# A hybrid pooling and short-convolution block on one core: the order of the branch units, a product by way of DRAM, and two Strassen steps more

## The chip, the cores and the metric

The kernel runs on one core of one Trainium2 chip. The metric is the device time of one execution in microseconds (us); lower is better. The engines are named as in the profile: PE (TensorE, matrix products), DVE (VectorE), ACT (ScalarE), POOL (GpSimd) and SP (SyncE); the last two issue transfers here, and POOL does little else.

## The reference

256 tokens, a model width of 4096, all in float32. The weights are read once and dominate the data (about 470 MB for the input, branch and output products).

```
h    = rmsnorm(x, norm_w)
proj = h @ w_in                      # 4096 -> 20480, split into u_p, z_p, u_c, b_c, c_c, z_c, g_logit
y_pool = causal_multiscale_pool(u_p) * silu(z_p)     # 2048 channels
y_conv = causal_gated_shortconv(u_c, b_c, c_c) * silu(z_c)   # 2048 channels
br     = [y_pool @ w_branch[0], y_conv @ w_branch[1]]        # each 2048 -> 4096
gates  = sigmoid(g_logit + gate_b)                   # two gates of 4096
merged = gates[0] * br[0] + gates[1] * br[1]
out    = rmsnorm(x + merged @ w_out, final_norm_w)
```

## The kernel before

**Units and steps.** Every large product is cut into units of 1024 output columns. A unit goes through its input channels in steps of 256 channels: 16 steps for the input and the output products, 8 steps for a branch product. A step loads 1 MB of weights into one of three `raw` buffers (SP issues the load), splits them into a high and a low part in the `ring` (ACT rounds the high part, DVE subtracts to get the low part), and multiplies by the standing operand, which lies in the `arena` in the same two parts. A product of two numbers is three matmuls: high by high, high by low, low by high.

**Two kinds of step.** A `P` step is the plain 2 by 2 block product: 8 block products, 24 matmuls of 128x512. An `S` step is one level of a Strassen scheme: 7 block products, 21 matmuls. It needs four sums of weight blocks as well (`parts`, made on DVE and split like the weights), and its products go to four more PSUM banks (`shared`, beside `sums`). When the unit ends, ACT copies those four into the tile `J` and DVE makes corner sums of them (`corner_sums`: three instructions), and the sums are added into the unit's result, `E` or `Y` (`combine`). A string of `P` and `S` sets the kinds and their order in each unit: `TEN`, for example, has ten `S`.

**How the corners are added.** Where `u.late` is set, POOL adds `J` to the result by two accumulating transfers (`gather`); otherwise DVE adds them, `E<-E,J` for a branch unit.

**The ring.** It has 15 cells of 512 columns. A `P` step takes 4 cells, an `S` step 3 and then 4 more for the sums. A cell comes free when PE has done its last matmul with it. So DVE and ACT work about two steps ahead of PE.

**What sets the order.** All engines run their instructions in the order in which the program is written (`pin` keeps it). After each group of matmuls, `pump` writes the preparation of later steps, and every 6 matmuls is a tick: one item is taken from a `queue`, which holds the epilogue of the unit before (`epi`, with `None` for an empty tick), and fills of standing operands may move on (`pop_fill`: POOL fetches a piece into `sa`, `sb` or `sc`, DVE and ACT make the operand of it).

**Branch units.** `b0_c` is gate column block c of branch zero, `b1_c` of branch one, c from 0 to 3. The order is b0_0, b1_0, b0_1, b1_1, b0_2, b1_2, b0_3, b1_3. `b0_c` ends with `Y = E * Y`, where Y held gate zero. `b1_c` ends with `E = E * gate one` (line 722; gate one lies in the tile `last_pair`, which the program calls `spare()`), `E = E + Y`, eight transposes of E on PE in each of two ticks, and a store of the turned result to `m_d[c]`, which the output units read. The gates of c = 0 stay in SBUF, the others are fetched from `gates_d`. The unit after b1_c thus carries its epilogue: in its first PE steps stand the transposes, which wait for the DVE instruction `E<-E,Y`.

**What the change touches.** The unit g1_0 (the last of the input product, text `SEVEN3`), `branch_unit` and the loop that makes the branch units.

Of the kernel before, what the change touches and what calls it, by code (L numbers as in the profile page):

```python
# [9 lines left out]
F32 = mybir.dt.float32  # L10
# [5 lines left out]
P = 128  # L16
# [3 lines left out]
NU = 1024  # L20
NH = 512
# [12 lines left out]
SIX5 = "PPPPPSPSPSPSPSPS"  # L34
FIRST = (0, 1, 8, 2, 9, 3, 10, 11, 4, 12, 13, 5, 14, 6, 15, 7)
OPENED = 12
SEVEN3 = "PPPSPSPSPSPSPSPS"
NINE = "PSPSPSPSSPSPSSPS"
NINE_A = "PSPSSPSPSSPSPSPS"
NINE_P = "PSPSSPSPSSPSSPSP"  # L40
HOST = "PPBPPMMPSSPSSPSSPSS"
TEN = "PSPSSPSSPSSPSSPS"
OUT3 = "PSPSPSPSPSPSSPPP"
B0 = "PPPPSPSP"
B1 = "PSPSPSPP"
B1_FIRST = "PPSPSPSP"
B0_MORE = "PPPPSSPS"


@with_exitstack  # L50
def hybrid_block(ctx: ExitStack, tc: tile.TileContext, x, xc, prm, rows_in, w_in, pool_w, w_branch, w_out, out):
# [5 lines left out]
    def act(dst, src, func=AF.Copy, **kw):  # L57
        return pin(nc.scalar.activation(dst, src, func, **kw))  # L58

    def tt(dst, a, b, op):  # L60
        return pin(nc.vector.tensor_tensor(out=dst, in0=a, in1=b, op=op))  # L61

    def mul(dst, a, b):
        return tt(dst, a, b, ALU.mult)

    def add(dst, a, b):
        return tt(dst, a, b, ALU.add)
# [13 lines left out]
    def move(dst, src):  # L81
        return pin(nc.gpsimd.dma_start(dst, src))

    def gather(dst, src):
        return pin(nc.gpsimd.dma_start(dst, src, accum_op=ALU.add))  # L85
# [5 lines left out]
    dram = ctx.enter_context(tc.tile_pool(name="dram", bufs=1, space=bass.MemoryType.DRAM))  # L91

    def sb(name, shape, dt=F32):
        return upper.tile(shape, dt, name=name)

    def blocks(name, shape, dt=F32):
        return const.tile(shape, dt, name=name)
# [4 lines left out]
    E = blocks("E", [P, 2, NU])  # L102
    sa = blocks("sa", [P, 8, P])
    J = blocks("J", [P, 4, NH])
    ident = blocks("ident", [P, P])
    raw = sb("raw", [P, NRAW, 2 * NU])
    Y = sb("Y", [P, 2, NU])
# [10 lines left out]
    gates_d = dram.tile([2, 4, P, 2, NU], F32, name="gates_d")  # L118
    g_d = dram.tile([2, P, 2, NU], F32, name="g_d")
    side_d = dram.tile([2, P, 2, 4, P], F32R, name="side_d")  # L120
    y_d = dram.tile([2, 2, P, 4, 2, T], F32, name="y_d")
    m_d = dram.tile([4, P, 4, 2, T], F32, name="m_d")
    o_d = dram.tile([3, P, 2, NU], F32, name="o_d")

# [28 lines left out]
    def open_last(dt):  # L153
        stack = ExitStack()
        ctx.enter_context(stack)
        pool = stack.enter_context(tc.tile_pool(name="last", bufs=1, side="right"))
        last_pair.update(stack=stack, tile=pool.tile([P, 8 * KB], dt, name="last_pair"))
# [87 lines left out]
    def quarters(tile_):  # L245
        return tile_.rearrange("p a (b c) -> p (a b) c", c=NH)
# [154 lines left out]
    def shared(i):  # L401
        return PF[i]
# [52 lines left out]
    def transposes(src, done):  # L455
        items = []
        for j in range(4):
            def f(j=j):
                for i in range(2):
                    for t in range(2):  # L460
                        c = (2 * j + i) * P
                        pin(nc.tensor.transpose(shared(j)[:, i * T + t * P:i * T + (t + 1) * P],  # L462
                                                src[:, t, c:c + P], ident))
                done(j)
            items.append(f)
        return items

    def pairs(items):
        return [lambda a=a, b=b: (a(), b()) for a, b in zip(items[::2], items[1::2])]

    def put(dst, src):
        for k in range(2):
            move(dst[:, :, 1 - k], src.rearrange("p (q k) t -> p q k t", k=2)[:, :, k])

    def chan(tile_):
        return tile_.rearrange("p a n -> p (a n)").rearrange("p (b t) -> p b t", t=T)

    def bankview(j):
        return shared(j).rearrange("p (b t) -> p b t", t=T)

    def gap(n):
        return [None] * n
# [36 lines left out]
    def seq_y(text):  # L519
        return sequence(text, 8 - text.count("S"), 8, 0)  # L520

    def in_unit(name, col, epi, text, **kw):
        units.append(Unit(name, lambda i: w_in[col // NU, i], seq_x(text), x_ops, epi, scaled=True, **kw))
        units[-1].text = text
        return units[-1]
# [20 lines left out]
    def rescale(d):  # L546
        return gap(18) + [lambda: act(d[:, 0], d[:, 0], scale=rin[:, 0:1]), None,
                          lambda: act(d[:, 1], d[:, 1], scale=rin[:, 1:2])]
# [142 lines left out]
    def gate_unit(n, c):  # L691
        first, final = (n, c) == (0, 0), (n, c) == (1, 0)

        def epi(u):
            d = u.dst

            def bias(t):
                gather(d[:, t], gate_b[n, None, c * NU:(c + 1) * NU].to_broadcast([P, NU]))

            def gate(t):  # L700
                act((spare() if final else d)[:, t], d[:, t], AF.Sigmoid)

            items = (rescale(d) if u.late else gap(1)) + [lambda: bias(0), lambda: bias(1)] + gap(12) + [
                lambda: gate(0), None, lambda: gate(1)]
            return items if first or final else items + [lambda: move(gates_d[n, c], E)]
        text = HOST if first else SEVEN3 if final else TEN
        u = in_unit(f"g{n}_{c}", 6 * HALF + n * D + c * NU, epi, text, dst=Y if first else E)
        u.late = not final

    def spare():  # L710
        return last_pair["tile"].rearrange("p (a n) -> p a n", a=2)

    def branch_unit(n, c):
        def epi(u):
            if n == 0:
                if c:
                    return gap(10) + [lambda: move(spare(), gates_d[1, c])] + gap(8) + [lambda: mul(Y, E, Y)]
                return gap(8) + [lambda: mul(Y, E, Y)]
            turned = spare() if c < 3 else Y

            def gated():
                mul(E, E, spare())
                if c == 3:
                    last_pair["stack"].close()
                    open_last(F32R)
                    last_pair["again"] = True

            def copy(j):
                act(chan(turned)[:, 2 * j:2 * j + 2], bankview(j))

            def stored():
                put(m_d[c], chan(turned))
                merged[c] = now[0] + STORED
            return gap(2) + [gated, None, lambda: add(E, E, Y), None,
                lambda: c < 3 and move(Y, gates_d[0, c + 1])] + gap(4) + pairs(transposes(E, copy)) + [stored]

        text = (B1 if c else B1_FIRST) if n else B0_MORE if c else B0
        u = Unit(f"b{n}_{c}", lambda i: w_branch[n, c, i], seq_y(text), y_ops[n], epi)
        u.late = n == 0 and c > 0
        if not u.late:  # L740
            u.urgent, u.lead = (lambda: None), 3
        units.append(u)
# [86 lines left out]
    for c in range(2):  # L829
        pool_units(c)  # L830
    gate_unit(0, 0)
    for c in range(1, 4):
        for n in range(2):
            gate_unit(n, c)
    gate_unit(1, 0)
    last_x = units[-1]
    for c in range(4):
        branch_unit(0, c)
        branch_unit(1, c)
    for c in range(4):  # L840
        out_unit(c)

# [126 lines left out]
    def done(i):  # L969
        steps[i].prepared = True  # L970
# [184 lines left out]
    for st in lead:  # L1155
# [7 lines left out]
        if not combined and last.closed(FB):  # L1163
            combined = True
            flush()
            rest = sums.rearrange("p (t a) n -> p t (a n)", t=2)
# [80 lines left out]
```

## Time and profile before

| what | value |
|---|---|
| median of 3 runs | 2356.45 us (2356.26 to 2356.69) |
| the profiled execution | 2356.82 us, of which the span of the instructions is 2354.7 us |
| PE busy | 2340.7 us (99%), 10,424 matmuls |
| DVE busy | 2217.8 us (94%) |
| ACT busy | 1542.9 us (66%) |
| POOL busy | 139.0 us (6%) |
| DMA | 569.44 MB, mean 242 GB/s |

In the rows of the profile, L61 is every DVE tensor-by-tensor operation, L58 every ACT operation, L82 and L85 the plain and the accumulating transfers of POOL, L1026 the matmuls of the steps and L462 the transposes. A row of the timeline gives the start, the time, the engine, the line and `out<-in`; in square brackets stand the idle time before it and what ended it. Two DVE rows that follow each other overlap by about 0.08 us in the records, so a piece's cost is taken from start to start.

### The profile page before, as it was taken

What the parts mean: (1) busy time and instruction counts of PE and PEld (TensorE: products, weight loads), DVE (VectorE), ACT (ScalarE), POOL (GpSimd) and SP (SyncE); (2) the same over time, 40 slices, a digit from 0 to 9 for tenths busy, and PEclk for the clock granted to TensorE, in tenths of its full rate; (3) what the DMA queues carried; (4) which work ended last, traced back from release to release, by engine and by line L of the source; (5) the groups of instructions that cost most, each with busy time, mean ns of one, the idle gap of its engine ahead of it and who ended that gap; (6) DMA issues with size and microseconds to landing.
All of it is one profiled execution on the core that took longest, in us unless ns stands there. A gap on an engine that the chain in (4) does not pass through costs nothing.

```text
span 2354.7 us, 28337 instructions
## 1 busy us (share of the span) xinstructions
PE 2340.7 (99%) x10424; PEld 1938.7 (82%) x10424; DVE 2217.8 (94%) x2454; ACT 1542.9 (66%) x1841; POOL 139.0 (6%) x195
## 2 busy tenths in 40 slices
PE   9999999999999999999999999999999999999998
PEld 7888888888888888888888888888888888888886
DVE  8899989999979979979999999998999899999998
ACT  6666756766656666666677767677666566566664
POOL 0000000000001000100000000001101001000000
PEclk9999999999999999999999999999999999999999
DMA  9667655776656656656787787778767678767877
GB/s 351 231 234 248 217 201 215 251 232 233 222 207 216 219 196 213 220 198 222 242 258 254 256 265 246 250 267 283 258 225 247 254 247 282 250 206 263 260 255 279
DMA packets 95387, 569.44 MB, mean 242 GB/s; under 512 B 10320, under 2 KB 10576, under 8 KB 34832
## 3 DMA queue, kind: packets, MB, share of 16 engines
q1 hardware_dynamic: 69824, 485.39, 56.7%
q0 software_dynamic: 24848, 81.01, 13.7%
q8 instruction: 81, 1.33, 0.2%
q10 hardware_dynamic: 576, 1.24, 0.1%
q14 instruction: 58, 0.48, 0.1%
HBM read 521.46 MB, written 25.17 MB: 232 GB/s over the span
## 4 chain that ended last, share of the span: by engine, by line
PE 97%; DVE 1%; DMA 0%; ACT 0%; issue 0%; DVEq 0%; SPq 0%; ACTq 0%
PE sums L1026 70%; PE shared L1026 25%; PE shared L676 1%; PE shared L462 1%; DVE ring L61 1%; DMA raw<-in_w_branch_dram 0%; DVE parts L61 0%; DMA raw<-in_w_in_dram 0%; ACT ring L58 0%; DVE arena L61 0%; PE shared L652 0%; DVE J L61 0%; ACT E L58 0%; PE shared L653 0%; PE shared L655 0%
## 5 line engine op out<-in xcount | busy, mean ns | idle before, releaser
L1026 PE MATMUL sums<-ring,arena 128*128 128x512 f32 x7011 | 1640.7, 390 | 1.9 <-ACT E L58 1.1
L1026 PEld LDWEIGHTS sums<-ring,arena 128*128 128x128 f32 x7011 | 1315.3, 188 | 275.5 <-ACT E L58 1.5
L61 DVE TENSOR_TENSOR ring<-raw,ring 128x1024 fp32r<-128x1024 f32 (+2 forms) x887 | 962.2, 1104 | 70.4 <-ACT ring L58 69.5
L58 ACT ACTIVATE ring<-raw 128x1024 fp32r<-128x1024 f32 (+3 forms) x682 | 785.5, 1192 | 210.2 <-PE sums L1026 98.5
L58 ACT ACTIVATE ring<-parts 128x512 fp32r<-128x512 f32 (+1 forms) x683 | 510.4, 761 | 510.2 <-DVE parts L61 438.3
L1026 PE MATMUL shared<-ring,arena 128*128 128x512 f32 x2241 | 541.1, 389 | 0.0
L61 DVE TENSOR_TENSOR ring<-parts,ring 128x1024 fp32r<-128x1024 f32 (+1 forms) x475 | 524.5, 1146 | 8.7 <-ACT ring L58 8.7
L1026 PEld LDWEIGHTS shared<-ring,arena 128*128 128x128 f32 x2241 | 420.6, 188 | 87.3
L61 DVE TENSOR_TENSOR parts<-parts,raw 128x512 f32<-128x512 f32 x444 | 303.3, 683 | 0.0
L61 DVE TENSOR_TENSOR parts<-raw 128x1024 f32<-128x1024 f32 x222 | 270.2, 1217 | 10.9 <-DMA raw<-in_w_in_dram 6.0
L61 DVE TENSOR_TENSOR J<-J 128x512 f32<-128x512 f32 (+1 forms) x90 | 78.1, 868 | 6.0 <-ACT J L58 2.8
L1026 PE MATMUL sums<-ring,last_pair 128*128 128x512 f32 x306 | 76.2, 389 | 0.0
L58 ACT ACTIVATE J<-shared 128x512 f32<-128x512 f32 x128 | 69.5, 601 | 1.6
L1026 PEld LDWEIGHTS sums<-ring,last_pair 128*128 128x128 f32 x306 | 57.4, 188 | 11.9
L85 POOL DMA_DIRECT2D E<-J x28 | 34.2, 1463 | 479.5 <-ACT ring L58 300.1
L1026 PE MATMUL shared<-ring,last_pair 128*128 128x512 f32 x216 | 51.9, 389 | 0.0
L1026 PE MATMUL shared<-ring,side 128*128 128x512 f32 x207 | 50.7, 389 | 0.0
L1026 PEld LDWEIGHTS shared<-ring,last_pair 128*128 128x128 f32 x216 | 40.5, 188 | 8.4
L1026 PEld LDWEIGHTS shared<-ring,side 128*128 128x128 f32 x207 | 38.9, 188 | 8.1
L58 ACT ACTIVATE E<-sums 128x512 f32<-128x512 f32 x76 | 41.8, 592 | 4.5 <-PE sums L1026 2.7
L85 POOL DMA_DIRECT2D Y<-J x12 | 14.7, 1458 | 265.1 <-ACT ring L58 138.5
L58 ACT ACTIVATE E<-sums,rin 128x512 f32<-128x512 f32 x20 | 13.0, 689 | 13.9 <-PE sums L1026 13.9
(140 smaller groups left out, 645.6 us busy)
## 6 DMA issues: line engine op xcount, KB each, us to landing
raw<-in_w_in_dram SPq DMA_DIRECT2D x318, 1024.0 KB, 4.9
raw<-in_w_branch_dram SPq DMA_DIRECT2D x64, 1024.0 KB, 5.4
raw<-in_w_out_dram SPq DMA_DIRECT2D x64, 1024.0 KB, 4.8
E<-J POOLq DMA_DIRECT2D x28, 512.0 KB, 8.6
E<-in_rows_dram POOLq DMA_DIRECT2D x14, 512.0 KB, 9.8
Y<-J POOLq DMA_DIRECT2D x12, 512.0 KB, 9.3
gates_d<-E POOLq DMA_DIRECT2D x6, 1024.0 KB, 6.1
y_d<-E POOLq DMA_DIRECT2D x8, 512.0 KB, 5.2
```

The costliest lines, as they stand in the source:

```text
L58: return pin(nc.scalar.activation(dst, src, func, **kw))
L61: return pin(nc.vector.tensor_tensor(out=dst, in0=a, in1=b, op=op))
L85: return pin(nc.gpsimd.dma_start(dst, src, accum_op=ALU.add))
L462: pin(nc.tensor.transpose(shared(j)[:, i * T + t * P:i * T + (t + 1) * P], src[:, t, c:c + P], ident))
L676: pin(nc.tensor.matmul(o, a, b, start=(k, i) == (0, 0), stop=(k, i) == (3, 2)))
L1026: pin(nc.tensor.matmul(ps, lhs, rhs, start=n == 0, stop=n == u.total[b] - 1))
```

## The change

The unit g1_0 gets eight `S` steps in place of seven. The branch units run in the order b0_0, b0_1, b1_0, b1_1, b0_2, b1_2, b0_3, b1_3. All units of branch zero, b0_0 now among them, take the text PPPPSSPS and have their corners added by transfers; b0_0 had PPPPSPSP, so it has three `S` in place of two. b1_0 changes from PPSPSPSP to PSPSPSPP, and b1_1 from PSPSPSPP to PPPPSSPS, each with three `S` as before. The first product of branch zero is stored to a new DRAM tile `p_d` while b0_1 runs, and Y takes gate zero of c = 1 after it. b1_0's epilogue loads `p_d` into J and adds J where it added Y. Gate one of c = 1 is fetched at the end of that epilogue, and no longer during b0_1.

```diff
-SEVEN3 = "PPPSPSPSPSPSPSPS"
+EIGHT3 = "PPPSPSPSSPSPSSPS"
...
-B0 = "PPPPSPSP"
 B1 = "PSPSPSPP"
-B1_FIRST = "PPSPSPSP"
-B0_MORE = "PPPPSSPS"
+B_LATE = "PPPPSSPS"
...
+    p_d = dram.tile([P, 2, NU], F32, name="p_d")
...
-        text = HOST if first else SEVEN3 if final else TEN
+        text = HOST if first else EIGHT3 if final else TEN
...
     def branch_unit(n, c):
         def epi(u):
             if n == 0:
-                if c:
-                    return gap(10) + [lambda: move(spare(), gates_d[1, c])] + gap(8) + [lambda: mul(Y, E, Y)]
-                return gap(8) + [lambda: mul(Y, E, Y)]
+                product = gap(18) + [lambda: mul(Y, E, Y)]
+                if c == 0:
+                    return product + [None, lambda: move(p_d, Y), lambda: move(Y, gates_d[0, 1])]
+                if c > 1:
+                    product[10] = lambda: move(spare(), gates_d[1, c])
+                return product
...
-            return gap(2) + [gated, None, lambda: add(E, E, Y), None,
-                lambda: c < 3 and move(Y, gates_d[0, c + 1])] + gap(4) + pairs(transposes(E, copy)) + [stored]
-
-        text = (B1 if c else B1_FIRST) if n else B0_MORE if c else B0
+            head = gap(2) + [gated, None, lambda: add(E, E, Y), None,
+                             lambda: c < 3 and move(Y, gates_d[0, c + 1])] + gap(4)
+            rest = []
+            if c == 0:
+                head = [lambda: move(J, p_d.rearrange("p a (b n) -> p (a b) n", n=NH)), None, gated] + gap(4) + [
+                    lambda: add(quarters(E), quarters(E), J)] + gap(3)
+                rest = gap(7) + [lambda: move(spare(), gates_d[1, 1])]
+            return head + pairs(transposes(E, copy)) + [stored] + rest
+
+        text = B1 if n and c != 1 else B_LATE
         u = Unit(f"b{n}_{c}", lambda i: w_branch[n, c, i], seq_y(text), y_ops[n], epi)
-        u.late = n == 0 and c > 0
+        u.late = n == 0
...
-    for c in range(4):
-        branch_unit(0, c)
-        branch_unit(1, c)
+    for n, c in ((0, 0), (0, 1), (1, 0), (1, 1), (0, 2), (1, 2), (0, 3), (1, 3)):
+        branch_unit(n, c)
```

The rows below are the program's order as it is built, without times; `x2` is the same row twice. First VectorE where the unit after b1_1, which is b0_2 in both kernels, begins. `J<-J` are b1_1's corner sums, `E<-E,J` adds them, `E<-E,last_pair` is the product with gate one, `parts` and the rows between belong to b0_2's first `S` step, and `E<-E,Y` is what the transposes wait for. Before:

```order
L61 TENSOR_TENSOR J<-J 128x512 x2
L61 TENSOR_TENSOR J<-J 128x1024
L61 TENSOR_TENSOR ring<-raw,ring 128x4x512 x2
L61 TENSOR_TENSOR E<-E,J 128x2048
L61 TENSOR_TENSOR ring<-raw,ring 128x4x512
L61 TENSOR_TENSOR E<-E,last_pair 128x2048
L61 TENSOR_TENSOR parts<-raw 128x1024
L61 TENSOR_TENSOR ring<-raw,ring 128x512
L61 TENSOR_TENSOR parts<-parts,raw 128x512
L61 TENSOR_TENSOR ring<-raw,ring 128x2x512
L61 TENSOR_TENSOR parts<-parts,raw 128x512
L61 TENSOR_TENSOR E<-E,Y 128x2048
```

The same place on VectorE now:

```order
L59 TENSOR_TENSOR ring<-raw,ring 128x4x512 x2
L59 TENSOR_TENSOR J<-J 128x512 x2
L59 TENSOR_TENSOR J<-J 128x1024
L59 TENSOR_TENSOR E<-E,J 128x2048
L59 TENSOR_TENSOR ring<-raw,ring 128x4x512
L59 TENSOR_TENSOR E<-E,last_pair 128x2048
L59 TENSOR_TENSOR parts<-raw 128x1024
L59 TENSOR_TENSOR ring<-raw,ring 128x512
L59 TENSOR_TENSOR parts<-parts,raw 128x512
L59 TENSOR_TENSOR ring<-raw,ring 128x2x512
L59 TENSOR_TENSOR parts<-parts,raw 128x512
L59 TENSOR_TENSOR E<-E,Y 128x2048
```

b1_1 ended in two `P` steps and ends in an `S` step now: its corner sums moved behind the preparation of two of b0_2's `P` steps, and from `E<-E,J` on the rows are the same. The place of the transposes on PE is the same too, 69 matmuls into b0_2.

Then POOL's queue from b0_0's end to b1_1's, before:

```order
L82 DMA Y<-gates_d 128x2048
L82 DMA m_d<-last_pair 512x1x256 x2
L82 DMA sa<-m_d 128x512
L82 DMA sb<-m_d 128x512
L82 DMA sc<-m_d 128x512
L85 DMA E<-J 128x2x512 x2
L82 DMA last_pair<-gates_d 128x2048
L82 DMA Y<-gates_d 128x2048
```

The same stretch of POOL's queue now:

```order
L83 DMA E<-J 128x2x512 x2
L80 DMA p_d<-Y 128x2048
L80 DMA Y<-gates_d 128x2048
L83 DMA E<-J 128x2x512 x2
L80 DMA J<-p_d 128x2048
L80 DMA m_d<-last_pair 512x1x256 x2
L80 DMA sa<-m_d 128x512
L80 DMA sb<-m_d 128x512
L80 DMA last_pair<-gates_d 128x2048
L80 DMA sc<-m_d 128x512
L80 DMA Y<-gates_d 128x2048
```

New are b0_0's two accumulating transfers, the store of the product and the load of it into J; the fetch of gate one moved behind the store of `m_d[0]`.

## The prediction

> **What bounds the kernel now.** I read the page first: engine shares, then the chain that ended last.
>
> ```profile
> PE 2340.7 (99%) x10424; PEld 1938.7 (82%) x10424; DVE 2217.8 (94%) x2454; ACT 1542.9 (66%) x1841; POOL 139.0 (6%) x195
> PE 97%; DVE 1%; DMA 0%; ACT 0%; issue 0%; DVEq 0%; SPq 0%; ACTq 0%
> ```
>
> PE is on the path nearly everywhere. A busy PE need not be at its pace, so I took that from the busy times by stretch, one stretch per unit from its first matmul to the next unit's: g1_1, g1_0, b0_0, b1_0, b0_2.
>
> ```profile
> core 0: us, PE busy (x) PEld busy (x) DVE busy (x) ACT busy (x) POOL busy (x), PEclk, DMA share, GB/s
> 1191.43:1271.67 80.24, 80.24 (x356) 66.44 (x354) 80.17 (x90) 56.51 (x69) 5.29 (x6) 1.00 0.80 258
> 1592.63:1674.91 82.28, 82.28 (x365) 68.13 (x363) 74.89 (x87) 55.69 (x66) 10.28 (x15) 1.00 0.84 275
> 1674.91:1718.30 43.39, 42.32 (x188) 34.72 (x186) 41.66 (x51) 31.20 (x39) 5.06 (x8) 1.00 0.80 263
> 1718.30:1759.95 41.65, 41.65 (x183) 34.47 (x184) 40.69 (x44) 27.27 (x34) 0.00 (x0) 1.00 0.55 202
> 1844.73:1888.03 43.30, 43.30 (x200) 36.01 (x199) 37.79 (x37) 25.85 (x33) 2.06 (x3) 1.00 0.67 242
> ```
>
> g1_1 has 10 S and 6 P, 10 x 21 + 6 x 24 = 354 matmuls in 80.24 us: 226.7 ns each. g1_0's 363 take 82.28 us, the same pace, without a gap. b0_0's 186 would take 42.16 us and take 43.39, b1_0's 183 would take 41.48 and take 41.65. So the branch part loses 1.23 + 0.17 = 1.40 us at one place, which PE's waits name (in us, times, longest), the only one of them behind the program's first 6 us:
>
> ```profile
> PE sums L1026 <- ACT E L58: 1.1, 1, 1.1
> ```
>
> It is the start of b1_0; the timeline of ACT and PE there:
>
> ```profile
> 1715.76 1.49 ACT L58 ACTIVATE ring<-raw 128x1536 fp32r<-128x1536 f32 x1 [1.29 <-DMA raw<-in_w_branch_dram]
> 1717.15 0.61 ACT L58 ACTIVATE arena<-sb 128x512 fp32r<-128x512 f32 x1
> 1717.67 2.04 ACT L58 ACTIVATE E<-sums 128x512 f32<-128x512 f32 x4
> 1718.30 1.45 PE L1026 MATMUL sums<-ring,arena 128*128 128x512 f32 x5 [1.07 <-ACT E L58]
> ```
>
> b0_0 ends in a P step, which closes its four `sums` banks together; their copies stood on ACT behind a piece that had waited for a load.
>
> So a reduction of work elsewhere than on PE is worth nothing. The change can gain only its matmuls and this wait, and lose whatever wait it makes.
>
> **The matmuls.** Two units trade a P for an S: 2 x (24 - 21) = 6 matmuls x 226.7 ns = -1.36 us.
>
> **The old wait.** b0_0 now ends in an S, in which the `sums` banks close up to a whole step before the end, and b0_1 follows. Taken as gone: -1.40 us; nothing saved if it comes back.
>
> **What the trades cost DVE.** The timeline of DVE at the start of b0_2, after b1_1, which has all pieces:
>
> ```profile
> 1845.56 2.29 DVE L61 TENSOR_TENSOR E<-E,J 128x2048 f32<-128x2048 f32 x1 [0.46 <-ACT E L58]
> 1848.24 2.29 DVE L61 TENSOR_TENSOR ring<-raw,ring 128x2048 fp32r<-128x2048 f32 x1 [0.39 <-ACT ring L58]
> 1850.45 2.29 DVE L61 TENSOR_TENSOR E<-E,last_pair 128x2048 f32<-128x2048 f32 x1
> 1852.65 1.22 DVE L61 TENSOR_TENSOR parts<-raw 128x1024 f32<-128x1024 f32 x1
> ...
> 1856.73 2.28 DVE L61 TENSOR_TENSOR E<-E,Y 128x2048 f32<-128x2048 f32 x1
> 1858.93 2.35 DVE L61 TENSOR_TENSOR ring<-parts,ring 128x1024 fp32r<-128x1024 f32 x2
> 1861.20 1.21 DVE L61 TENSOR_TENSOR parts<-raw 128x1024 f32<-128x1024 f32 x1
> ```
>
> From start to start, a P's preparation is 2.2 us, and an S's 1856.73 - 1852.65 = 4.1 for the sums and 1861.20 - 1858.93 = 2.3 for their split, 6.4 together: +4.2 us of DVE per trade. In g1_0 DVE is busy 74.9 of 82.3 us, so 7.4 us of idle time take it; g1_1 keeps PE's pace with ten S and DVE at 80.17 of 80.24. Cost in g1_0: 0.
>
> In b0_0 it is closer. g1_0's own epilogue and six fills fall there; DVE's timeline at its start:
>
> ```profile
> 1677.90 2.29 DVE L61 TENSOR_TENSOR ring<-raw,ring 128x2048 fp32r<-128x2048 f32 x1 [1.20 <-ACT ring L58]
> 1680.11 2.67 DVE L61 TENSOR_TENSOR J<-J 128x512 f32<-128x512 f32 x3
> 1682.81 2.48 DVE L73 SCALAR_TENSOR_TENSOR E<-J,rin,E 128x1024 f32<-128x1024 f32 x2
> 1685.21 1.22 DVE L61 TENSOR_TENSOR ring<-raw,ring 128x1024 fp32r<-128x1024 f32 x1
> ```
>
> And the groups of the fills' pieces (count, busy time, mean ns):
>
> ```profile
> L61 DVE TENSOR_TENSOR sa<-sa 128x128 f32<-128x128 f32 x68 | 16.6, 286 | 0.8 <-ACT sa L58 0.2
> L61 DVE TENSOR_TENSOR arena<-sa,arena 128x896 fp32r<-128x896 f32 x11 | 12.0, 1089 | 0.2
> L61 DVE TENSOR_TENSOR arena<-sa,arena 128x512 fp32r<-128x512 f32 x7 | 4.8, 682 | 0.0
> ```
>
> DVE is done with the third P's piece 5.2 us after b0_0's first matmul (1674.91). The 1.2 us of idle time before it, ended by ACT, show that DVE was not late, so the extra S of g1_0 doesn't move it. From there, in the new order up to the sums of the last S: corners and their addition 5.1 (1680.11 to 1685.21), two P 4.4, three S 19.1, and fills: twelve small sums at 16.6 / 68 = 0.24, two pieces of 0.6, one of 1.0 and one of 1.1 (a `parts` row above): 6.2. Together 5.2 + 34.8 = 40.0 us. PE needs the last of these sums in the third product of that step: 4 x 24 + 2 x 21 + 24 + 7 = 169 matmuls, 38.3 us. A wait of 1.7; 0.7 if ACT, which has one fill piece less to do ahead of that P than in the trace, lets DVE start 1 us sooner. Bounds 0 and 2.0; I take +0.8, near the sooner start, whose cause stands in the built order.
>
> **The new wait: b0_2's transposes.** In the rows above, b1_1's corner sums were over before b0_2 began (they are not in the list), `E<-E,J` ended at 1847.85, 3.1 us after b0_2's first matmul at 1844.73, and `E<-E,Y` at 1859.01, 14.3 us after it. The transposes follow:
>
> ```profile
> 1842.69 17.85 PE L1026 MATMUL sums<-ring,arena 128*128 128x512 f32 x78
> 1860.38 1.03 PE L462 MATMUL shared<-ident,E 128*128 128x128 f32 x8
> ```
>
> They start 15.65 us after it (69 matmuls), 1.4 us after DVE was done. b1_1 now ends in an S, whose `shared` banks close last: its corner sums come after two P pieces of b0_2, as g1_0's stand behind those of b0_0 in the trace. There the corners are over 1682.81 - 1674.91 = 7.9 us into the unit, since the second P's rounding on ACT stands between the copies of `J`:
>
> ```profile
> 1674.44 0.65 ACT L58 ACTIVATE arena<-sb 128x512 fp32r<-128x512 f32 x1
> 1674.96 1.10 ACT L58 ACTIVATE J<-shared 128x512 f32<-128x512 f32 x2
> 1675.92 1.95 ACT L58 ACTIVATE ring<-raw 128x2048 fp32r<-128x2048 f32 x1
> 1677.72 1.11 ACT L58 ACTIVATE J<-shared 128x512 f32<-128x512 f32 x2
> ```
>
> Without that fill (0.5) and with slightly shorter copies of `E` I take 7.1. Then `E<-E,J` 2.2, a P 2.2, gate one 2.2, the sums of the S 4.1, `E<-E,Y` 2.3: 20.1. PE waits 20.1 - 15.65 = 4.4 us. Bounds: 3.2, if the corners begin as soon as ACT's last copy is done (3.2, and 2.7 for them, so 5.9), and 5.2 with g1_0's 7.9. Nothing hides it: PE has no idle time to give back.
>
> **The transfers.** The issues (count, KB each, median us from issue to landing):
>
> ```profile
> gates_d<-E POOLq DMA_DIRECT2D x6, 1024.0 KB, 6.1
> Y<-gates_d POOLq DMA_DIRECT2D x3, 1024.0 KB, 5.6
> last_pair<-gates_d POOLq DMA_DIRECT2D x3, 1024.0 KB, 17.6
> ```
>
> The product of b0_0 comes 18 ticks (24.5 us) into b0_1 at the earliest, say at 30. Store 6.1 and load of Y 5.6 on POOL: 42. Behind them in the queue stand b0_1's own `E<-J`, which have no corners before 46, and Y is read 24 us into b1_0: 0, with 20 us of cover. `J<-p_d` can start when `E<-E,J` is done, 3.1 us into b1_1 (P ends b1_0, as it ended b1_1 above), and lands near 9; DVE comes to its `E<-E,J` at 12, and the transposes at 72 matmuls, 16.3, leave 2.0 more. Cost 0 as long as the load takes under 10.5 us. The fills of y for b1_0 have a unit more. The addition in b1_0's epilogue replaces another; b0_0's corners leave DVE (2.2 us) for transfers that end long before tick 18.
>
> **Sum.** -1.36 - 1.40 + 0.8 + 4.4 = +2.4 us. The profiled execution took 2356.82 us around its span of 2354.7, 0.37 over the median of 2356.45, to which I apply the sum: 2358.9 us, +0.10%. A measurement of this kernel tells about 0.2% from no change, 4.7 us: 2351.7 to 2361.2. Faster than that is not in PE's reach, as only 2.8 us can be gained.
>
> **Rivals.** *No new wait.* If b1_1's corners are done as early as after a P, the 1.4 us of slack stay: 2356.45 - 2.76 = 2353.7. Against it: the S closes those banks last, and g1_0 shows 7.9 us. 8%.
>
> *The stall stops the clock.* The busy times at the program's end (the granted clock is the third number from the right):
>
> ```profile
> 2335.00:2344.00 9.00, 8.72 (x39) 6.89 (x37) 7.24 (x16) 3.54 (x8) 0.00 (x0) 1.00 0.32 130
> 2344.00:2349.00 5.00, 0.00 (x0) 0.00 (x0) 4.17 (x11) 2.08 (x4) 0.00 (x0) 0.94 0.67 270
> 2349.00:2354.00 5.00, 0.00 (x0) 0.00 (x0) 0.00 (x0) 0.00 (x0) 0.00 (x0) 0.50 0.87 356
> ```
>
> And PE's timeline at its start:
>
> ```profile
> 5.98 6.35 PE L1026 MATMUL sums<-ring,arena 128*128 128x512 f32 x18 [0.83 <-DVE ring L774]
> ```
>
> PE ends at 2343.7; a mean of 0.94 over 5 us is 0.6 us at half clock, so it fell at 2348.4, 4.7 us after the last matmul. And 18 matmuls at the start took 6.35 us where they take 4.2 at pace: 2.1 us lost. If the stall at the transposes reaches 4.7 us (its upper bound is 5.2), the clock falls and PE restarts slowly: 2356.45 - 2.76 + 0.8 + 5.2 + 2.1 = 2361.8, slower. Against it: my 4.4 is below, and the wait of 1.07 us at 1718 left the clock at 1.00. 13%. [...]
>
> *J comes late.* At 17.6 us, as `last_pair<-gates_d`, it lands 21.1 into b1_1, DVE's addition ends at 23.4 and PE waits 7.1 more: 2366. Against it: those loads stood behind two accumulating transfers, and this one has none ahead. 4%.
>
> *DVE falls behind by more in g1_0 or b0_0.* For it: in b0_0 the running sum has no idle time left, so any delay there is PE's. Against it: g1_1 holds the pace with ten S. 3 us over my sum would be 2361.9. 5%.
>
> **Chances and range.** The forecast has 70%; its own range is 2356.45 - 2.76 + 3.2 = 2356.9 to 2356.45 - 2.76 + 2.0 + 5.2 = 2360.9. The range 2355.5 to 2361.9 leaves out the case without a wait, the late J and the upper halves of the clock and DVE cases. Faster 1%; within 0.2% the forecast and the first rival, 78%; slower 21%.
>
> **What would show it.** Right: the unit g1_0 at 360 x 226.7 ns = 81.6 us; no wait for `E<-sums` copies at the unit after b0_0; PE waiting for DVE's `E` 3 to 5 us ahead of the transposes in b0_2, with `E<-E,Y` ending near 20 us into it; under 2 us of waiting for DVE's `ring` at b0_0's last S; J landing 9 us into b1_1. Wrong: transposes in b0_2 that wait for nothing, a wait in b1_1, or a granted clock under 1.00 after the stall.

## The result, and the profile after

| | before | after |
|---|---|---|
| median, same chip | 2356.82 us (2356.09 to 2357.91, 10 runs) | 2362.82 us (2362.36 to 2365.21, 10 runs) |
| ratio to before | | 1.0026, 95% interval 1.0018 to 1.0034 |
| profiled execution, span | 2356.82, 2354.7 us | 2362.69, 2361.0 us |

The change makes the kernel 6.0 us slower; +2.4 was forecast. (Two single executions in the experiments, one of e12 with 3972.29 us and one of the kernel before beside it with 4827.55 us, are left out of all numbers.) In the kernel after, the step matmuls stand at L1033, the transposes at L461, DVE's operations at L59 and ACT's at L56. PE's waits (us in total, times, longest) first; the row of `ring` at L59 also holds a wait in the first 20 us:

```profile
PE shared L461 <- DVE E L59: 4.3, 1, 4.3
PE sums L1033 <- DVE ring L59: 2.8, 2, 1.8
PE sums L1033 <- ACT E L56: 1.0, 1, 1.0
```

The busy times by stretch, one stretch per unit: g1_0, b0_0, b0_1, b1_0, b0_2 (columns as in the prediction):

```profile
1593.13:1674.73 81.60, 81.60 (x361) 67.57 (x360) 78.45 (x92) 57.77 (x68) 10.29 (x15) 1.00 0.84 266
1674.73:1718.64 43.91, 41.95 (x185) 34.08 (x183) 41.99 (x53) 29.41 (x35) 4.34 (x7) 1.00 0.73 241
1718.64:1760.56 41.92, 41.90 (x184) 34.38 (x185) 40.93 (x44) 28.63 (x36) 4.30 (x6) 1.00 0.89 287
1760.56:1802.04 41.48, 41.48 (x185) 34.35 (x184) 39.04 (x37) 27.34 (x32) 2.44 (x2) 1.00 0.81 267
1845.34:1894.70 49.36, 45.11 (x200) 37.24 (x199) 42.37 (x42) 28.16 (x35) 2.02 (x3) 0.97 0.62 216
```

g1_0 is 0.68 us shorter, as 3 matmuls of 226.7 ns should make it. A branch unit of three `S` that waits for nothing takes 41.48 (b1_0); the transposes bring it to 43.30. So b0_0 loses 2.43 us, b0_1 0.44 and b0_2 6.06. That b0_2's granted clock is 0.97, not 1.00, is the second thing to see.

DVE at the start of b0_2, then PE there:

```profile
1849.65 2.67 DVE L59 TENSOR_TENSOR J<-J 128x512 f32<-128x512 f32 x3
1852.36 2.29 DVE L59 TENSOR_TENSOR E<-E,J 128x2048 f32<-128x2048 f32 x1
...
1856.77 2.28 DVE L59 TENSOR_TENSOR E<-E,last_pair 128x2048 f32<-128x2048 f32 x1
1858.97 1.21 DVE L59 TENSOR_TENSOR parts<-raw 128x1024 f32<-128x1024 f32 x1
...
1863.06 2.28 DVE L59 TENSOR_TENSOR E<-E,Y 128x2048 f32<-128x2048 f32 x1
```

```profile
1845.34 15.80 PE L1033 MATMUL sums<-ring,arena 128*128 128x512 f32 x69
1865.39 1.66 PE L461 MATMUL shared<-ident,E 128*128 128x128 f32 x8 [4.25 <-DVE E L59]
```

The corners end 7.0 us into the unit (7.1 forecast), `E<-E,Y` 20.0 (20.1), and the transposes start 4.4 us later than 69 matmuls would let them. The rest of the 6.06, 1.66 us, is the clock. The busy times in three stretches of 3.41 us that begin within the stall (the granted clock is the third number from the right):

```profile
1862.35:1865.76 3.41, 0.37 (x3) 0.37 (x4) 3.41 (x4) 2.00 (x2) 0.12 (x1) 1.00 0.42 120
1865.76:1869.17 3.41, 3.41 (x13) 2.92 (x12) 3.41 (x4) 1.19 (x2) 0.42 (x1) 0.50 0.98 382
1869.17:1872.58 3.41, 3.41 (x21) 2.88 (x20) 3.41 (x6) 2.25 (x5) 1.10 (x2) 1.00 0.29 120
```

PE was idle for 3.04 of the first stretch, ran at half clock through the whole second one and at full clock from the third.

At the end of b0_0 there are two waits. PE, ACT and DVE there:

```profile
1714.16 0.73 PE L1033 MATMUL sums<-ring,arena 128*128 128x512 f32 x2 [0.95 <-DVE ring L59]
...
1718.64 1.71 PE L1033 MATMUL sums<-ring,arena 128*128 128x512 f32 x5 [1.01 <-ACT E L56]
```

```profile
1712.47 0.94 ACT L56 ACTIVATE arena<-sb 128x896 fp32r<-128x896 f32 x1
...
1715.20 0.62 ACT L56 ACTIVATE arena<-sa 128x512 fp32r<-128x512 f32 x1
...
1718.01 1.55 ACT L56 ACTIVATE E<-sums 128x512 f32<-128x512 f32 x3
```

```profile
1706.75 1.01 DVE L59 TENSOR_TENSOR sb<-sb 128x128 f32<-128x128 f32 x4
...
1711.76 2.35 DVE L59 TENSOR_TENSOR ring<-parts,ring 128x1024 fp32r<-128x1024 f32 x2
```

The sums of the last `S` end 1711.76 + 2.35 - 1674.73 = 39.4 us into b0_0 and PE waits for them. Then the copies of E stand on ACT behind two fill pieces, and PE waits for those at b0_1's start: the old wait is back at the same boundary. The load of the stored product cost nothing. Its row in the list of issues (count, KB, us from issue to landing), and DVE's addition, 12.0 us into b1_1, which began at 1802.04:

```profile
J<-p_d POOLq DMA_DIRECT2D x1, 1024.0 KB, 5.6
```

```profile
1814.03 2.28 DVE L59 TENSOR_TENSOR E<-E,J 128x2048 f32<-128x2048 f32 x1
```

### The profile page after: what moved, and what is told of

It reads as the page before. It is cut to its first block, busy times and chain, and to the rows that moved or that the text cites. A ratio compares the mean times of both kernels' runs of the same rounds, so it can differ in the third digit from the quotient of the medians.

```text
span 2361.0 us, 28358 instructions
## 1 busy us (share of the span) xinstructions
PE 2339.8 (99%) x10418; PEld 1937.0 (82%) x10418; DVE 2224.5 (94%) x2468; ACT 1545.9 (65%) x1847; POOL 142.5 (6%) x199
## 4 chain that ended last, share of the span: by engine, by line
PE 97%; DVE 1%; ACT 1%; DMA 1%; issue 0%; SPq 0%; DVEq 0%; ACTq 0%
PE sums L1033 69%; PE shared L1033 25%; PE shared L675 1%; PE shared L461 1%; DMA raw<-in_w_in_dram 1%; DVE ring L59 1%; ACT ring L56 0%; DVE E L59 0%; DVE parts L59 0%; PE shared L651 0%; DVE J L59 0%; ACT E L56 0%; ACT last_pair L56 0%; ACT arena L56 0%; PE shared L652 0%
## 5 line engine op out<-in xcount | busy, mean ns | idle before, releaser
L1033 PE MATMUL sums<-ring,arena 128*128 128x512 f32 x6996 | 1637.0, 390 | 4.8 <-DVE ring L59 2.8
L1033 PEld LDWEIGHTS sums<-ring,arena 128*128 128x128 f32 x6996 | 1311.5, 188 | 278.5 <-DVE ring L59 3.7
L59 DVE TENSOR_TENSOR ring<-raw,ring 128x1024 fp32r<-128x1024 f32 (+2 forms) x893 | 962.2, 1097 | 69.4 <-ACT ring L56 68.5
L56 ACT ACTIVATE ring<-raw 128x1024 fp32r<-128x1024 f32 (+3 forms) x681 | 784.7, 1193 | 199.8 <-PE sums L1033 83.0
L56 ACT ACTIVATE ring<-parts 128x512 fp32r<-128x512 f32 (+1 forms) x690 | 515.3, 760 | 523.3 <-DVE parts L59 457.8
L1033 PE MATMUL shared<-ring,arena 128*128 128x512 f32 x2253 | 544.0, 389 | 0.0
L59 DVE TENSOR_TENSOR ring<-parts,ring 128x1024 fp32r<-128x1024 f32 (+1 forms) x478 | 529.3, 1149 | 8.8 <-ACT ring L56 8.8
L1033 PEld LDWEIGHTS shared<-ring,arena 128*128 128x128 f32 x2253 | 422.9, 188 | 87.8
L59 DVE TENSOR_TENSOR parts<-parts,raw 128x512 f32<-128x512 f32 x448 | 306.2, 683 | 0.0
L59 DVE TENSOR_TENSOR parts<-raw 128x1024 f32<-128x1024 f32 x224 | 272.8, 1218 | 11.3 <-DMA raw<-in_w_in_dram 6.4
L59 DVE TENSOR_TENSOR J<-J 128x512 f32<-128x512 f32 (+1 forms) x90 | 78.1, 868 | 5.9 <-ACT J L56 2.8
L1033 PE MATMUL sums<-ring,last_pair 128*128 128x512 f32 x291 | 72.8, 389 | 0.0
L56 ACT ACTIVATE J<-shared 128x512 f32<-128x512 f32 x128 | 69.6, 605 | 1.3
L1033 PEld LDWEIGHTS sums<-ring,last_pair 128*128 128x128 f32 x291 | 54.6, 188 | 11.4
L1033 PE MATMUL shared<-ring,last_pair 128*128 128x512 f32 x228 | 54.8, 389 | 0.0
L1033 PE MATMUL shared<-ring,side 128*128 128x512 f32 x207 | 50.7, 389 | 0.0
L1033 PEld LDWEIGHTS shared<-ring,last_pair 128*128 128x128 f32 x228 | 42.8, 188 | 8.9
L56 ACT ACTIVATE E<-sums 128x512 f32<-128x512 f32 x76 | 41.8, 593 | 6.9 <-PE sums L1033 5.1
L1033 PEld LDWEIGHTS shared<-ring,side 128*128 128x128 f32 x207 | 38.9, 188 | 8.1
L80 POOL DMA_DIRECT2D y_d<-E x8 | 6.1, 805 | 270.5 <-ACT E L56 147.8
```

Source lines behind the costliest of these rows:

```text
L1033: pin(nc.tensor.matmul(ps, lhs, rhs, start=n == 0, stop=n == u.total[b] - 1))
```

## The experiments

All ratios are to the kernel before, run on the same chip (medians 2356.4 to 2356.9 us). The kernel after is 2362.82, where the kernel before ran at 2356.82; as the medians of before differ by 0.5 us, comparisons of a time with 2362.82 hold to about that.

**e1: the transposes three ticks later.**

```diff
-                             lambda: c < 3 and move(Y, gates_d[0, c + 1])] + gap(4)
+                             lambda: c < 3 and move(Y, gates_d[0, c + 1])] + gap(7 if c == 1 else 4)
```

> The changed kernel with the transposes of b1_1's result three ticks (18 matmuls, 4.1 us) later in b0_2; nothing else moves. Theory: the wait for DVE's E<-E,Y (4.41 us in the changed kernel) is what fell on PE, and the half clock behind it (1.66 us more in b0_2 than the wait) is a consequence of the wait. Then the wait falls to 0.3 us or less, the granted clock in b0_2 stays at 1.00, b0_2 takes about 43.5 us in place of 49.37, and the kernel is 5.7 us below the changed one: about 2357.1. Rival: the slow stretch behind the transposes has a cause of its own (the transposes themselves, or loads and copies that collide there); then only the 4.1 us of the wait goes, the clock drops all the same, and the time is about 2358.7.

2358.57 us (2358.24 to 2358.87), ratio 1.0007 (0.9998 to 1.0015). PE in b0_2:

```profile
1865.17 1.09 PE L461 MATMUL shared<-ident,E 128*128 128x128 f32 x8 [0.17 <-DVE E L59]
...
1872.73 2.33 PE L1033 MATMUL shared<-ring,arena 128*128 128x512 f32 x9 [1.43 <-ACT last_pair L56]
```

The time is the rival's, but not its mechanism. The wait went to 0.17, the clock stayed at 1.00 (in the stretches from 1865 to 1870 and from 1870 to 1875 us), and a wait that neither side had named took 1.43 us: the transposes use the `shared` banks, ACT's copies out of them now come just when the first `S` needs the banks, and one pair of them stands behind `ring<-parts`, which waits for DVE:

```profile
1871.56 0.63 ACT L56 ACTIVATE ring<-parts 128x512 fp32r<-128x512 f32 x1 [1.16 <-DVE parts L59]
1872.10 1.07 ACT L56 ACTIVATE last_pair<-shared 128x512 f32<-128x512 f32 x2
```

**e2: one tick later.** As above with `gap(5)`.

> The changed kernel with the same transposes one tick (6 matmuls, 1.36 us) later. DVE's end doesn't move, so the wait should go from 4.41 to about 3.05 us. Theory A (the clock halves only after a stretch of about 3.4 us in which PE is almost idle, as the 3.413 us at half clock in the changed kernel suggest): a wait of 3.05 us is too short, b0_2 loses 1.36 and the 1.66 us of half clock besides, and the time is about 2359.8 with the granted clock at 1.00. Theory B (any stall of a few microseconds lets the clock fall, or each costs in proportion): the drop stays, and the time is about 2361.4.

2359.91 us (2359.35 to 2363.97), ratio 1.0015 (1.0006 to 1.0024): theory A. The wait was 2.89 us. The busy times in three stretches of the profiled execution, cut 3.41 us apart:

```profile
1860.48:1863.90 3.42, 2.25 (x10) 1.52 (x9) 3.42 (x5) 2.13 (x3) 0.00 (x0) 1.00 0.24 98
1863.90:1867.31 3.41, 1.69 (x12) 1.56 (x13) 3.41 (x3) 2.56 (x4) 0.54 (x1) 1.00 0.75 283
1867.31:1870.72 3.41, 3.41 (x21) 2.88 (x20) 3.41 (x5) 2.23 (x6) 0.59 (x1) 1.00 0.83 334
```

The stall is shared out over two stretches, 1.2 and 1.7 us, and the clock stays. 7 of 11 executions lay within 2359.35 to 2359.93 with a granted clock of 0.999, the others up to 4 us above with 0.996 to 0.998.

**c1: the clock by itself.** A kernel that only stalls PE, with lengths set by a DVE operation:

```diff
+    for r in range(ROUNDS):
+        for q, (n, width) in enumerate(WIDTHS):
+            tt(seen, acc[1 - k][:, 0:P], src[:, 0:P])
+            tt(far[:, 0:width], src[:, 0:width], src[:, 0:width])
+            tt(w[n], src[:, 0:512], src[:, 512:1024])
+            burst(n, 44 + (7 * r + 3 * q) % 15)
```

> Not the kernel, but the clock by itself: bursts of 44 to 58 matmuls of 128x512 with a wait for DVE ahead of each, in ten lengths that repeat fourteen times (from about 1.2 to about 5.5 us); the result of the block isn't computed, and its time is of no use. Theory A (the clock is set at fixed boundaries 3.413 us apart, by whether PE idled through the whole stretch between two): stalls under 3.4 us never lower it, stalls of 4.4 us in about 3 of 10 cases. Theory B (a stretch that is idle for a part is enough; the changed kernel showed a drop where 89% of one was idle): stalls of 4.4 us lower it in most cases, and some of 3 us too. Theory C (any stall above a fixed length lowers it, at once): a sharp limit between two lengths, and the drop begins at no fixed boundary. In all, one drop costs about half of the 3.413 us, 1.7, as seen in the changed kernel.

PE's waits, one row for a length (the row of `wa` has the start's 9.6 us besides):

```profile
PE acc L42 <- DVE wj L31: 74.4, 14, 5.3
...
PE acc L42 <- DVE wg L31: 50.2, 14, 3.6
PE acc L42 <- DVE wf L31: 42.7, 14, 3.1
...
PE acc L42 <- DVE wa L31: 29.9, 15, 9.6
PE acc L42 <- DVE wb L31: 27.8, 14, 2.0
```

The trace's clock record, set beside these, gives how many of 14 stalls of each length were followed by half clock. The last row is the mean time of a matmul in the bursts behind stalls of that length, in ns; over the whole run the granted clock was 0.89:

| stall, us | 1.45 | 2.0 | 2.25 | 2.5 | 2.8 | 3.05 | 3.6 | 4.1 | 4.7 | 5.3 |
|---|---|---|---|---|---|---|---|---|---|---|
| half clock after | 0 | 9 | 8 | 9 | 12 | 10 | 14 | 14 | 14 | 14 |
| mean of a matmul, ns | 395 | 417 | 414 | 415 | 423 | 420 | 440 | 442 | 439 | 445 |

The busy times in four stretches of 3.41 us at one stall of 5.32 us, which ended at 172.04 (PE, PEld, DVE and POOL; the granted clock is again the third number from the right):

```profile
166.62:170.03 3.41, 0.10 (x1) 0.00 (x0) 3.27 (x2) 0.00 (x0) 1.00 0.00 0
170.03:173.45 3.42, 1.41 (x3) 1.16 (x4) 1.96 (x2) 0.00 (x0) 0.50 0.00 0
173.45:176.86 3.41, 3.41 (x9) 2.64 (x8) 0.00 (x0) 0.00 (x0) 0.50 0.00 0
176.86:180.27 3.41, 3.41 (x16) 2.79 (x15) 0.00 (x0) 0.00 (x0) 1.00 0.00 0
```

PE was idle for 3.31 us of the first stretch and 2.01 of the second; the second and the third ran at half clock, the fourth, after a stretch without idle time, at full clock. So theory B: half clock followed 9 of 14 stalls of 2.0 us, 22 of the 28 of 2.8 and 3.05 us and all of 3.6 us and more. Theory A, which has none under 3.4 us, is too mild, and no one length parts the two outcomes, which theory C has. The kernel after has 4.4 us, between 4.1 and 4.7 with 14 of 14 each. In e2 theory A hit its number, in a profiled execution with 1.2 and 1.7 us of the stall in two stretches. Of the 28 stalls of 2.8 and 3.05 us here 6 left the clock as it was, but in e2 7 of 11 executions kept 0.999. Why so many did there stays open.

**e3: the two fills behind b0_0.**

```diff
+                ok = freed(i)
+                if n == 1 and i.region in (("q", 1), ("u", 0)):
+                    ok = lambda ok=ok: ok() and names["b0_0"].flags.get("base")
```

> The changed kernel with the last two fills of branch one's operand (their sums on DVE and ACT, about 3 us of DVE) held back until b0_0 has written its last steps, so that they no longer stand ahead of the sums of b0_0's last S. Theory: both waits around b0_0's end (1.12 us for DVE's sums in the last S, 1.17 us for ACT's copies of E at the start of b0_1, with 0.43 us of slower restart) come from DVE being late in b0_0, the second because ACT's pieces of the last S stood behind DVE's parts. Then both go, b0_0 takes about 41.5 us in place of 43.90, and the time is about 2360.2 (2.4 to 2.8 us below the changed kernel). Rival: ACT's copies at the start of b0_1 are late for a reason of their own (the old wait of 1.07 us at that unit boundary, only renamed); then only the first goes, -1.1 us: about 2361.7.

2361.12 us (2360.28 to 2363.47), ratio 1.0017 (1.0008 to 1.0026). b0_0, then three stretches in b0_2:

```profile
1676.35:1718.16 41.81, 41.78 (x185) 34.27 (x184) 39.80 (x47) 28.32 (x33) 3.97 (x6) 1.00 0.75 253
```

```profile
1860.68:1864.09 3.41, 0.02 (x1) 0.00 (x0) 3.41 (x4) 1.91 (x4) 0.00 (x0) 1.00 0.16 26
1864.09:1867.50 3.41, 2.55 (x10) 2.43 (x11) 3.41 (x4) 2.12 (x3) 0.53 (x1) 0.50 0.93 346
1867.50:1870.92 3.42, 3.42 (x14) 2.85 (x12) 3.42 (x5) 0.60 (x2) 0.00 (x0) 0.50 0.60 249
```

Both waits went: b0_0 takes 2.10 us less, b0_1 0.16 less, b1_0 0.20 more. That is 2.06 us, and the median fell by 1.7. The profiled execution is the slowest of the eleven (2363.47): in b0_2 the stall, unchanged at 4.25, cost half clock through two stretches, of which the first still held 0.86 us of the stall, and b0_0 began 1.62 us later than in the kernel after (1676.35 against 1674.73). How many stretches the other executions lost isn't shown. The same stall cost 1.66 us more in the kernel after and 50.59 - 43.30 - 4.4 = 2.9 here: one stretch at half clock there, two here.

**e12: one fill.** That run took pieces from DVE and from ACT; this one takes only the one that stands ahead of ACT's copies, `i.region == ("q", 1)` in the condition above.

> The changed kernel with only one of the two fills of e3 held back: the one whose pieces (arena<-sa: 0.62 us on ACT, 0.6 on DVE) stand behind the sums of b0_0's last S on DVE, and ahead of the copies of E on ACT. The other fill (sb: 1.0 us of small sums on DVE ahead of the last S, 0.94 on ACT) stays. Theory A: the wait in the last S is due to DVE's sb sums and stays at 1.12 us, while the wait at b0_1's start is due to what stands on ACT ahead of the copies, and falls by the 0.62 of the piece, from 1.17 to about 0.55: b0_0 takes about 43.3 us (43.90 in the changed kernel), the kernel about 2362.2. Theory B: both waits are due to DVE's lateness alone; then b0_0 stays at 43.9 and the time at 2362.8.

PE at the end of b0_0:

```profile
1713.97 0.74 PE L1033 MATMUL sums<-ring,arena 128*128 128x512 f32 x2 [0.95 <-DVE ring L59]
...
1717.93 3.31 PE L1033 MATMUL sums<-ring,arena 128*128 128x512 f32 x12 [0.45 <-ACT E L56]
```

Theory A: the first wait is unchanged at 0.95, the second fell from 1.01 to 0.45, b0_0 to 43.4. So 0.56 of the second wait is that piece on ACT, and not DVE, whose sums end as late as before. The kernel's median is 2362.47 us (2361.66 to 2362.86; ratio 1.0025, 1.0015 to 1.0035), no clear gain: in the profiled execution b0_2 took 50.2 us, 0.8 more than in the kernel after, with a mean granted clock of 0.52 in the 7 us from 1863: about two stretches at half clock again.

**e6: two S in b0_0.**

```diff
-        text = B1 if n and c != 1 else B_LATE
+        text = B1 if n and c != 1 else "PPPPSPSP" if (n, c) == (0, 0) else B_LATE
```

> The changed kernel with two S steps in b0_0 in place of three, PPPPSPSP in place of PPPPSSPS (the text before the change), ending in a P; 3 matmuls more (0.68 us), 4.2 us less of DVE. Theory (DVE late in b0_0 causes both waits there): the wait inside the last S goes (1.12 us); whether the wait at b0_1's start goes too depends on what ACT is behind: if it is only DVE's lateness it goes (1.17 and 0.43 us), b0_0 takes 42.2 us and the kernel about 2360.8. Rival (the copies of E on ACT are late after any P that closes four banks, as in the kernel before): that wait stays at 1.0 to 1.2 us and the time is about 2362.2.

2363.13 us (2362.87 to 2364.26), ratio 1.0028 (1.0017 to 1.0039): the rival. ACT and PE at b0_0's end, and PE late in o0, the first output unit:

```profile
1714.60 1.92 ACT L56 ACTIVATE ring<-raw 128x2048 fp32r<-128x2048 f32 x1 [1.12 <-DMA raw<-in_w_branch_dram]
1716.42 2.04 ACT L56 ACTIVATE E<-sums 128x512 f32<-128x512 f32 x4
```

```profile
1717.05 2.12 PE L1033 MATMUL sums<-ring,arena 128*128 128x512 f32 x8 [0.86 <-ACT E L56]
...
2101.49 0.73 PE L1033 MATMUL sums<-ring,arena 128*128 128x512 f32 x2 [1.07 <-DVE arena L59]
```

The wait in the last `S` is gone, the one at the boundary is of the kind of the kernel before: four copies behind a piece that waited for a load. And 1.07 us is lost in a place that the edit doesn't touch, which the next run shows as well.

**e4: the eighth S of g1_0 alone.** In the kernel before:

```diff
-SEVEN3 = "PPPSPSPSPSPSPSPS"
+SEVEN3 = "PPPSPSPSSPSPSSPS"
```

> The kernel before with one part of the change alone: g1_0 has eight S in place of seven. Theory: 3 matmuls fewer at 226.7 ns, hidden otherwise: g1_0 takes 81.6 us (82.28 before), b0_0 stays at 43.4, and the time is 0.7 us below the kernel before, about 2356.0. Rival: the 4.2 us more of DVE in g1_0 make b0_0 late, whose last S has no idle time of DVE ahead of it; then b0_0 takes 44 us or more and the time is as before or above, 2356.7 or more.

2358.46 us (2358.02 to 2359.99), ratio 1.0010 (1.0001 to 1.0019): slower than before: the rival, and more than it said. g1_0 is 0.68 shorter, b0_0 takes 44.20 (43.39 before) and o0 86.13 (84.78). These make 1.5 of the 2.1 us; in the profiled execution the rest lies ahead of g1_0, which the edit doesn't touch. PE at both places, DVE in o0, and DVE in o0 of the kernel before:

```profile
1719.10 3.24 PE L1026 MATMUL sums<-ring,arena 128*128 128x512 f32 x13 [1.88 <-ACT E L58]
...
2096.74 1.88 PE L1026 MATMUL sums<-ring,arena 128*128 128x512 f32 x7 [1.05 <-DVE arena L61]
```

```profile
2093.32 2.36 DVE L61 TENSOR_TENSOR ring<-raw,ring 128x1024 fp32r<-128x1024 f32 x2 [0.28 <-ACT ring L58]
2095.60 1.08 DVE L61 TENSOR_TENSOR arena<-sa,arena 128x896 fp32r<-128x896 f32 x1
```

```profile
2092.07 1.08 DVE L61 TENSOR_TENSOR arena<-sa,arena 128x896 fp32r<-128x896 f32 x1
2093.07 2.35 DVE L61 TENSOR_TENSOR ring<-raw,ring 128x1024 fp32r<-128x1024 f32 x2
```

The two DVE pieces have changed places, 420 us behind the edit. Fills move on at ticks, one per six matmuls; three matmuls fewer shift every later tick by half of one against the steps. Both kernels with three fewer in all (this and the one before it) wait there; those with six fewer, a whole tick, don't (o0 84.77 us after). That this shift is the cause is argued from these counts, not shown by a run of its own.

**e5: b1_1 ends in a P.**

```diff
-        text = B1 if n and c != 1 else B_LATE
+        text = "PPPPSSSP" if (n, c) == (1, 1) else B1 if n else B_LATE
```

> The changed kernel with only the order of steps in b1_1 changed, PPPPSSSP in place of PPPPSSPS: the unit ends in a P, as b1_1 did before the change; the number of matmuls is the same. Theory: it is the S at b1_1's end that makes its corners late (closed last, done about 7 us into b0_2), and so E<-E,Y and the transposes. With a P at the end the corners are done near the unit's end, E<-E,Y ends about 14.5 to 16 us into b0_2, the wait at the transposes is 0.5 us or less, the clock stays at 1.00, and the time is about 2356.8 (6.0 us below the changed kernel). Rival: the lateness comes from the new order of units (DVE is behind as a whole when two units of branch one follow each other), whatever b1_1 ends in; then a wait of 3 us or more stays and the time is above 2360.

2359.49 us (2358.90 to 2363.45), ratio 1.0013 (1.0005 to 1.0022). PE at b0_2's start and DVE's `E<-E,Y`:

```profile
1847.48 15.94 PE L1033 MATMUL sums<-ring,arena 128*128 128x512 f32 x69 [1.89 <-ACT E L56]
1863.26 1.03 PE L461 MATMUL shared<-ident,E 128*128 128x128 f32 x8
```

```profile
1859.87 2.29 DVE L59 TENSOR_TENSOR E<-E,Y 128x2048 f32<-128x2048 f32 x1
```

The transposes wait for nothing, so the `S` at b1_1's end was what made them late, and not the order of the units. But b1_1 now closes four banks in its last `P`, and ACT's copies of E stand behind a `ring<-raw` that had waited 3.50 us for PE: PE waits 1.89 us. That lies between the 1.45 us of c1, with no half clock after any of 14, and the 2.0 us, with 9 of 14, which fits the wide range; the profiled execution, the fastest, had a mean clock of 0.999. Of the 6.0 us forecast, 2.05 went into that wait (b1_1 took 45.35 us up to b0_2's first matmul, 43.30 in the kernel after).

**e10: E<-E,Y ahead of the sums.** One DVE instruction of b0_2 moved (the product with gate one is written a tick earlier too, but keeps its place among DVE's rows):

```diff
-            head = gap(2) + [gated, None, lambda: add(E, E, Y), None,
+            head = gap(1 if c == 1 else 2) + [gated] + gap(0 if c == 1 else 1) + [lambda: add(E, E, Y)] + gap(3 if c == 1 else 1) + [
```

> The changed kernel with one DVE instruction moved: in b0_2, E<-E,Y follows directly on E<-E,last_pair, ahead of the sums of the first S step (4.1 us of DVE) in place of behind them; nothing else moves on any engine. Theory: the 4.4 us wait came from the place of E<-E,Y in DVE's order behind late corners. It then ends 15.9 us into b0_2 where the transposes stand at 15.65, the wait is 0.5 us or less, no clock drop follows, and the sums, 2.3 us later than before, still come ahead of PE (their product stands about 25 us into the unit, their split ends near 22.3). b0_2 takes about 43.6 us, the kernel about 2357.0 (5.8 us below the changed one). Rival: the sums are now what is late; then the wait moves to the first S step, 2 us or more for DVE's ring, and the time is 2359 or above.

2356.91 us (2356.53 to 2358.52), ratio 1.0001 (0.9992 to 1.0010): the theory, to 0.1 us. PE and DVE:

```profile
1862.78 1.09 PE L461 MATMUL shared<-ident,E 128*128 128x128 f32 x8 [0.30 <-DVE E L59]
```

```profile
1860.44 2.29 DVE L59 TENSOR_TENSOR E<-E,Y 128x2048 f32<-128x2048 f32 x1
```

**e11: both edits.** E<-E,Y ahead of the sums, and the two fills behind b0_0.

> The edit of e10 (E<-E,Y ahead of the sums in b0_2) and that of e3 (two fills behind b0_0) together. Theory: the two losses of the changed kernel, in b0_0 and b0_1 (2.1 us by e3) and in b0_2 (5.8 us by e10's expectation), are separate and add up: 2362.8 - 7.9 = about 2354.9, below both kernels. Rival: the fills held back make DVE late in b1_0 or b1_1 and eat the gain; then 2356.5 or above.

2354.91 us (2354.25 to 2355.47), where the kernel before ran at 2356.66 (2356.12 to 2357.47): ratio 0.9992 (0.9983 to 1.0001). The two losses are separate and add up. It is the fastest of all that were run, 7.9 us under the kernel after; against the kernel before the runs don't overlap, but the interval just reaches 1.

## Why the prediction was wrong, point by point

The forecast of 2358.9 us was too low by 3.9, and 2362.82 lies above its range. By terms, from the profiled executions:

| term | forecast | measured |
|---|---|---|
| six matmuls | -1.36 | -1.36 |
| the old wait at the unit after b0_0 | -1.40 | +0.17 |
| b0_0's last S waits for DVE's sums | +0.8 | +1.2 |
| b0_2's transposes wait for E<-E,Y | +4.4 | +4.4 |
| half clock behind that wait | 0 | +1.66 |
| sum | +2.4 | +6.1 |

The start, the output units and what lies outside the span make up -0.27, and rounding the rest, to +5.87. A further 0.4 us of the miss is the base: 2356.45 from three runs, where ten gave 2356.82.

- **Right: the new wait.** Its place, its chain (corners late by the `S` at b1_1's end, then the rows of DVE in order) and its size. The runs with b1_1 ending in a P and with `E<-E,Y` ahead of the sums show that both links are needed.
- **Right: g1_0, the transfers of the stored product, DVE's late sums** (39.4 us against 40.0 or 39 forecast; the wait within its bounds of 0 and 2.0, half over the value taken).
- **Wrong: "the old wait" taken as gone.** The step said that the `sums` banks close early in an `S`, and left out what stands on ACT ahead of their copies. The wait came back whole, 1.57 us with the slow matmuls behind it, and one fill piece of 0.62 us less took 0.56 of it away. 1.6 us of the miss.
- **Wrong: the clock.** The rival had the mechanism and its place, at 13%, but the condition, that the stall "reaches 4.7 us", was read off the one drop at the program's end. In c1 half clock followed 14 of 14 stalls of each length from 3.6 us on, 4.1 and 4.7 among them. With that, the clock's price on top of the forecast, 2358.9 + 1.7 to 2.9, would have been the likeliest. The term that the sum put at 0 measured 1.66: 1.7 us of the miss. All ten executions lay at 2362.36 us or above, where some 2361.2 would be expected without the drop (2362.82 - 1.66).
- **Not foreseen: what a trade does far behind itself.** "Cost in g1_0: 0" held within g1_0, yet in e4 the same edit alone cost 2.2 us elsewhere (0.81 in b0_0, 1.35 in o0). In the change as a whole its part cannot be told apart from b0_0's other changes.

## What to carry to other kernels

When a unit is given a different last step, follow each of its closing banks through the queue of the engine that copies them, entry by entry, and then the first instruction of the next unit that needs the result: both losses here sat in such a queue, and moving one DVE instruction ahead of work that was not yet needed gave 5.9 us back. Price a stall of PE of 2.0 us or more with the risk of a stretch at half clock (9 of 14 at 2.0 us in c1; a stretch cost 1.7 us here, two 2.5 to 2.9), and one of 3.6 us or more with that cost (14 of 14 in c1). Where helpers are placed by counts of matmuls, a step saved anywhere re-times all that follows, so compare the built order to the end of the program.

## What the runs showed of the hardware

In the kernel after the granted clock was 0.50 for one stretch of 3.41 us and 1.00 on both sides of it; PE had been idle for 3.04 us of the stretch before. In c1, where the granted clock was 0.89 over the run, half clock followed none of 14 stalls of 1.45 us, 9 of 14 of 2.0 us and 14 of 14 of 3.6 us and more. One wait of PE, 4.4 us each time, cost 1.7, 2.9 and 2.5 us more in three kernels (after, e3, e12). A wait of PE for DVE's `ring` near 17 us, 1.82 us long in the profiled execution of after and absent before, left the clock at 1.00 there (17.50 to 30.00 us); the first unit took 89.5 us with it and 89.1 before. The profiled executions of e3 and e10 have a wait of 1.8 us for that tile too; b0_0 began 1.62 us later in e3 than in after, b0_2 1.34 us later in e10. The clock at that wait in these two isn't shown.
